# A one-core encoder layer: weights prepared twice are left out, two pairs share one raw tile, two sums move to VectorE

## The chip, the cores and the metric

The kernel runs on one core of one Trainium2 chip. The metric is the time of one execution on the device, in microseconds (us). Three executions of the kernel before took 1694.86, 1699.55 and 1696.46 us, so its median is 1696.46 us.

Five engines of the core have a part in it: TensorE (PE, matmuls, with its weight loads as PEld), VectorE (DVE), ScalarE (ACT), GpSimd (POOL) and SyncE (SP), which issues the DMAs. Each runs its own instructions strictly in their order and waits for others by semaphores.

## The reference

One layer of an encoder is computed for 1024 prompt rows and 128 sample rows (8 requests of 16): a mixer of a linear recurrence and a sliding-window attention, a cross attention into 256 memory tokens, and a feed-forward, each with a residual and a layer norm. The change touches only the last line of this:

```python
D_MODEL = 1024
D_FF = -(-8 * D_MODEL // (3 * 256)) * 256          # 2816

def swiglu(x, w_in, w_out):
    g, u = jnp.split(x @ w_in, 2, axis=-1)
    return (jax.nn.silu(g) * u) @ w_out

def post_blocks(x, mix, mk, mv, w_mem_q, w_mem_o, w_ffn_in, w_ffn_out, ln_g, ln_b):
    x = layer_norm(ALPHA * x + mix, ln_g[0], ln_b[0])
    x = layer_norm(ALPHA * x + mem_attention(x, mk, mv, w_mem_q, w_mem_o), ln_g[1], ln_b[1])
    x = layer_norm(ALPHA * x + swiglu(x, w_ffn_in, w_ffn_out), ln_g[2], ln_b[2])
    return x
```

Everything is float32.

## The kernel before

**Precision.** A float32 operand is split into a high part (a cast to the fp32r format, on ACT) and a low part (the operand less the high part, a subtraction). A product is three matmuls: high by high, high by low, low by high (`mm3`). So each operand of TensorE costs a cast on ACT and a subtraction on DVE or POOL, of 128x512 elements in the part that matters here.

**The feed-forward in 2x2 blocks.** Both its projections use the scheme of Strassen and Winograd: a product of 2x2 blocks takes seven block products in place of eight, and additions ahead and behind. The second projection multiplies the hidden values (2816 wide) by `w_f2`. The 2816 rows are 11 *pairs* of 256. Pair i of `w_f2` is one raw tile, 128x2x1024, loaded in two DMAs of 512 KB (L1124); its blocks A11, A12, A21, A22 are 128x512 each. Four sums S1 to S4 of these blocks are made on POOL (L1135, in `add`). Eight blocks (A11, A12, A21, A22, S1 to S4) are then split: the cast on ACT (L1147, in `upper`), the low part on DVE, or on POOL for A21 and A22 (L1153, in `lower`). The low and high parts of a pair fill four tiles `w2`. All this is "the preparation of pair i"; the results stay in the dictionary `prepared` until they are used.

**The hidden values** come out of the first projection as seven operands, B11, T1, T2, B22, T3, B21 and T4, are stored to a scratch in DRAM (L1049), and are loaded back as tiles `hq` (L1198), whose split is `hh` (ACT, L1207) and `hl` (L1208; DVE, or POOL for T1, T3, T4). Their last differences are L1082 (POOL) and L1090 (DVE, for the last pair). The sample rows' hidden values have their own way: tanh on ACT (L961), two operations on DVE (L962, L963).

**Parts and turns.** `PARTS = ((0, 2), (2, 4), (4, 6), (6, 8), (8, 11))` groups the pairs: part 0 holds pairs 0 and 1, and so on, the last part pairs 8, 9 and 10. The prompt rows are eight tiles of 128; tile b (0 to 3) and tile b+4 make the two rows of the 2x2 scheme, so there are four *blocks* of tiles. A part but the last runs a first *turn* over blocks 0 and 1, then the sample rows, then a second turn over blocks 2 and 3. The last part takes the blocks one at a time: 0, 1, the sample rows, 2, 3, and normalizes each block's rows as it ends (`final_norm`, L1095 to L1111). A turn runs seven steps, and each adds a product to a bank of PSUM:

```python
        steps = (("x", "A11", "B11", True, (0, 0, None)),
                 ("z", "S1", "T1", True, (1, 1, None)),
                 ("x", "S2", "T2", False, (1, 0, None)),
                 ("z", "S4", "B22", False, (1, 0, 1)),
                 ("x", "S3", "T3", False, (1, 1, 1)),
                 ("w", "A12", "B21", True, (0, 0, 0)),
                 ("x", "A22", "T4", False, (0, 1, 0)))
```

Behind each step an add on DVE (L1230) reads the bank into the result `y` and so frees the bank; the w products go through `tap` instead (ACT L1227, POOL L1228), except in the last part. There are two banks each of x, z, w and s (sample rows). TensorE cannot start a product into a bank that is not free.

**What is prepared when.** While part n runs, `plans` prepares the pairs of part n+1 in between. It returns two lists, `first` and `second`, one for each turn: what stands in slot z of a list is written behind step z of that turn. `put` fills them: `load` is the raw load, `a0` the sums S1 and S2, `a1` the sums S4 and S3, `u0` to `u3` the casts, `l0` to `l3` the low parts. In the last part the first of its two turns with a plan is block 1's. The framework then gives each engine its order, from the order in the code and its own view of when operands are ready; the rows below show what came out.

**Memory.** Pool `c` has 14 units of 128x2048 float32, shared by raw tiles, sums, `w2` tiles and a few others, and exists from the first projection on. Pool `f2` is opened with the second projection, over the memory of the first projection's tiles. It holds the results `y`, the `hq`, `hh` and `hl` tiles, and one raw tile, used by the second pair of each part (`k == 1` in `plans`). The raw tile of the first pair of each part is a unit of `c`, and may therefore be loaded before `f2` is there. A tile is loaded anew only when its last reader is through.

**One more thing in the last part.** Its branch loads the gains and offsets of the layer norm in a loop over `n`, the name that also numbers the parts:

```python
                for n in range(2):
                    nc.sync.dma_start(out=gb[n], in_=I["ln"][4 + n:5 + n, :].broadcast_to([P, D]))
            load_sample, part_sample, hx = sample_operands(part)
            first, second = plans(n, load_sample, part_sample)
```

Behind the loop n is 1, so `plans` works for part 2: pair 4 is loaded, summed and split once more, and pair 5's raw tile loaded once more. The last part doesn't use them, and `second` isn't run there.

The loads of `y` at the start are L1311, the store of the sample's hidden values L1314.

Of the kernel before, what the change touches and what calls it, by code (L numbers as in the profile page):

```python
# [18 lines left out]
P = 128  # L19
D = 1024  # L20
# [12 lines left out]
PAIRS = FT // 2  # L33
FILL = 5
PARTS = ((0, 2), (2, 4), (4, 6), (6, 8), (8, 11))
# [67 lines left out]
def trunk(ctx, tc, I, O):  # L103
    nc = tc.nc
    V, S, G = nc.vector, nc.scalar, nc.gpsimd
# [28 lines left out]
    def split(src, hi, lo, scale=None):  # L134
        if scale is None:
            S.copy(hi, src)  # L136
            V.tensor_tensor(lo, src, hi.bitcast(F32), op=ALU.subtract)  # L137
        else:
            S.activation(hi, src, AF.Copy, scale=scale)
            V.scalar_tensor_tensor(lo, src, scale, hi.bitcast(F32), op0=ALU.mult, op1=ALU.subtract)  # L140
# [88 lines left out]
    both = const.tile([P, 1280], F32, name="both")  # L229
# [689 lines left out]
    def unit(c, name, dt=F32):  # L919
        return c.tile([P, 2048], dt, name=name, tag="u", bufs=14)  # L920
# [192 lines left out]
    def second_weights(c):  # L1113

        prepared = {}

        def prepare(i, at):

            raw, sums, units, out = [], [], [], prepared.setdefault(i, {})

            def load():
                t = at().tile([P, 2, 1024], F32, name="raw2") if at else unit(c, "raw2").rearrange("p (n x) -> p n x", n=2)
                for n in range(2):
                    nc.sync.dma_start(out=t[:, n], in_=I["w_f2"][n, i])  # L1124
                raw.extend(t[:, n, x * 512:x * 512 + 512] for n in range(2) for x in range(2))

            def add(k):
                a11, a12, a21, a22 = raw
                if k == 0:
                    t = unit(c, "s2").rearrange("p (n x) -> p n x", x=512)  # L1130
                    sums.extend(t[:, n] for n in range(4))
                s1, s2, s3, s4 = sums
                for o, x, y, op in (((s1, a21, a22, ALU.add), (s2, s1, a11, ALU.subtract)),
                                    ((s4, a12, s2, ALU.subtract), (s3, a11, a21, ALU.subtract)))[k]:
                    G.tensor_tensor(o, x, y, op=op)  # L1135

            def names(k):
                a11, a12, a21, a22 = raw
                s1, s2, s3, s4 = sums
                return ((("A11", a11), ("S1", s1)), (("S2", s2), ("S4", s4)), (("S3", s3), ("A12", a12)),  # L1140
                        (("A22", a22), ("A21", a21)))[k]

            def upper(k):
                t = unit(c, "w2", F32R).rearrange("p (n x) -> p n x", x=512)
                units.append(t)
                for n, (_, src) in enumerate(names(k)):
                    S.copy(t[:, 2 * n], src)  # L1147

            def lower(k):
                t = units[k]  # L1150
                for n, (name, src) in enumerate(names(k)):
                    hi, lo = t[:, 2 * n], t[:, 2 * n + 1]
                    (G if name in ("A21", "A22") else V).tensor_tensor(lo, src, hi.bitcast(F32), op=ALU.subtract)  # L1153
                    out[name] = hi, lo

            return {"load": load, **{f"a{k}": (lambda k=k: add(k)) for k in range(2)},
                    **{f"u{k}": (lambda k=k: upper(k)) for k in range(4)},
                    **{f"l{k}": (lambda k=k: lower(k)) for k in range(4)}}

        def first_operands():  # L1160

            (i0, i1), out = PARTS[0], {}
            k = i1 - i0
            q = unit(c, "q2")[:, :k * 512].rearrange("p (o i b x) -> p o i b x", o=2, i=k, b=2)
            t = unit(c, "h2", F32R)[:, :k * 1024].rearrange("p (o y i b x) -> p o y i b x", o=2, y=2, i=k, b=2)
            for n, o in enumerate(OPS[:2]):
                nc.sync.dma_start(out=q[:, n], in_=h_dram[0, n, :, i0:i1])
                split(q[:, n], t[:, n, 0], t[:, n, 1])
                out[0, o] = [[(t[:, n, 0, i, b], t[:, n, 1, i, b]) for i in range(k)] for b in range(2)]
            return out  # L1170

        return prepared, prepare, first_operands

    def second_projection(f2, c, ahead, prepared, prepare):

        y = {}
        sums = [bank("s") for _ in range(2)]
        gb = []
# [14 lines left out]
        def load(n):  # L1193
            if n < len(wanted) and n not in loaded:
                i0, i1, bs, o = wanted[n]
                k, m, c = i1 - i0, len(bs), bs[0] % 2
                q = f2.tile([P, 512], F32, name="hq", bufs=5)[:, :k * m * P].rearrange("p (i b x) -> p i b x", b=m, x=P)
                nc.sync.dma_start(out=q, in_=h_dram[bs[0] // 2, OPS.index(o), :, i0:i1, c:c + m])  # L1198
                loaded[n] = q
# [81 lines left out]
        def plans(n, load_sample, part_sample):  # L1281


            first, second = [[] for _ in steps], [[] for _ in steps]
            first[2].append(load_sample)
            first[5].append(part_sample)
            if n + 1 < len(PARTS):
                nexts = [prepare(i, (lambda: f2) if k == 1 else None) for k, i in enumerate(range(*PARTS[n + 1]))]

                def put(plan, k, **at):  # L1290
                    for x, z in at.items():
                        plan[z].append(nexts[k][x])

                put(first, 0, load=0, a0=1, a1=2, u0=2, l0=3, u1=3, l1=4, u2=4, l2=5, u3=5, l3=6)
                put(first, 1, load=1)
                put(second, 1, a0=0, a1=0, u0=0, l0=1, u1=1, l1=2, u2=2, l2=3, u3=3, l3=4)
                if len(nexts) > 2:
                    put(second, 2, load=3, a0=5, a1=5, u0=5, l0=6, u1=6, l1=6, u2=6, l2=6, u3=6, l3=6)
            return first, second
# [4 lines left out]
        for n, part in enumerate(PARTS):  # L1304
            last = n == len(PARTS) - 1
            if n == 0:

                for k, (e, half) in enumerate(((0, 0), (1, 1), (1, 0), (0, 1))):
                    c2 = slice(half * 512, half * 512 + 512)
                    for b in range(2):  # L1310
                        nc.sync.dma_start(out=y[b, e][:, c2], in_=x2_dram[TILES[b + 4 * e]][:, c2])  # L1311
                    if k == 1:
                        load(0)
                nc.sync.dma_start(out=hs_dram[:, PAIRS - 1], in_=hs.rearrange("p (e t) -> p e t", e=2))  # L1314
            if last:
                both = unit(c, "ln_gb").rearrange("p (n x) -> p n x", n=2)
                gb = [both[:, n] for n in range(2)]
                for n in range(2):
                    nc.sync.dma_start(out=gb[n], in_=I["ln"][4 + n:5 + n, :].broadcast_to([P, D]))
            load_sample, part_sample, hx = sample_operands(part)  # L1320
            first, second = plans(n, load_sample, part_sample)
            for bs in ((0,), (1,)) if last else ((0, 1),):
                yield from blocks(part, bs, gb, first if bs[-1] == 1 else ())
            if n == 0:
                for e in range(2):
                    for b in range(2, 4):
                        nc.sync.dma_start(out=y[b, e], in_=x2_dram[TILES[b + 4 * e]])
            yield from sample(part, hx, n == 0, last)
            if last:
                ys = unit(c, "ys")[:, :1024]  # L1330
                nc.sync.dma_start(out=ys, in_=x2_dram[SAMPLE])
                bn = sm.tile([P, 2, 6], F32, name="bn", bufs=6)
                for half in range(2):
                    c2 = slice(half * 512, half * 512 + 512)
                    V.scalar_tensor_tensor(ys[:, c2], ys[:, c2], ALPHA, sums[half], op0=ALU.mult, op1=ALU.add)
                    V.bn_stats(bn[:, half], ys[:, c2])
                final_norm(ys, gb, bn, None, None)
                for b in (2, 3):
                    yield from blocks(part, (b,), gb)
                return  # L1340
            yield from blocks(part, (2, 3), gb, second)
# [211 lines left out]
```

## Time and profile before

| | us |
|---|---|
| median of three executions | 1696.46 |
| the profiled execution | 1701.0 |
| its span in the trace | 1699.2 |
| PE busy in the span | 1625.7 |
| first product of the second projection (PE, x, 12 matmuls) starts | 1381.49 |

The mean granted clock of TensorE over the span is 0.98 of full. The second projection takes the stretch from there to the end. A row of the timeline gives the start in us from the span's start, the duration, the engine, the line, the operation with output and inputs, the count, and in brackets how long the engine stood before it and what ended that. A row of windows gives the stretch and its length, then busy time and count of PE, PEld, DVE, ACT and POOL, that of SP's DMA issues, the granted clock of TensorE (1.00 is full), the busy share of the DMA engines and the GB/s. A row of groups gives the count, the busy time, the mean in ns, and the idle time before; a row that lists durations gives the shortest, median and longest of one instruction in ns, and the stretch over which they lie.

### The profile page before, as it was taken

How to read it: one execution, taken by the hardware profiler on the slowest of the kernel's cores; microseconds unless marked ns; L12 is line 12 of the kernel's file. 1: busy time of each engine (PE TensorE's matmuls, PEld its weight loads, DVE VectorE, ACT ScalarE, POOL GpSimd, SP SyncE). 2: the span in 40 equal slices, each digit the busy share in tenths (PEclk: the TensorE clock that was granted, in tenths of full speed). 3: DMA queues.
4: the chain of work that ended last, by engine and by line, in shares of the span. 5: the costliest groups of instructions: out<-in, count | busy, mean ns of one | idle time of the engine just before them, and what ended most of it. 6: DMA issues, size and time to landing. Idle time of an engine off the chain costs nothing.

```text
span 1699.2 us, 24497 instructions
## 1 busy us (share of the span) xinstructions
PE 1625.7 (96%) x9065; PEld 1397.4 (82%) x9065; DVE 1145.7 (67%) x2032; ACT 681.7 (40%) x1380; POOL 511.3 (30%) x389
## 2 busy tenths in 40 slices
PE   8999999999999999999999999999999979999894
PEld 7998999999888987889887888888888867777672
DVE  6886688788478666787687545544444576677766
ACT  4543455546433545134353333322322434334322
POOL 1111121111000000000057444323333455678556
PEclk9999999999999999999999999999999989999997
DMA  7453243333875588637364222322222256344431
GB/s 239 133 170 122 91 149 106 97 117 122 291 281 165 179 269 303 225 113 258 124 211 140 100 93 100 106 83 90 91 96 96 91 186 208 88 129 131 155 110 74
DMA packets 120679, 252.11 MB, mean 148 GB/s; under 512 B 12144, under 2 KB 63728, under 8 KB 120560
## 3 DMA queue, kind: packets, MB, share of 16 engines
q1 hardware_dynamic: 120560, 250.55, 44.3%
q8 instruction: 71, 1.16, 0.3%
q14 instruction: 48, 0.39, 0.1%
HBM read 207.84 MB, written 42.60 MB: 147 GB/s over the span
## 4 chain that ended last, share of the span: by engine, by line
PE 80%; DVE 7%; POOL 5%; DMA 4%; ACT 2%; issue 2%; SPq 1%; POOLq 0%; ACTq 0%; DVEq 0%
PE a L96 47%; PE b L96 20%; PE x L96 5%; PE z L96 3%; POOL s L1135 2%; PE b L100 2%; PE s L96 2%; DMA raw<-in_w_f_dram 2%; DVE w L1153 1%; PE w L96 1%; DVE T_l L940 1%; DMA w_raw<-in_w_mv_dram 1%; DVE sc L550 1%; DVE B_l L940 1%; DVE w_lo L137 0%
## 5 line engine op out<-in xcount | busy, mean ns | idle before, releaser
L137 DVE TENSOR_TENSOR w_lo<-w_raw,w_hi 128x1024 fp32r<-128x1024 f32 (+1 forms) x169 | 204.9, 1216 | 115.6 <-ACT w_hi L136 115.1
L136 ACT CAST w_hi<-w_raw 128x1024 fp32r<-128x1024 f32 (+1 forms) x169 | 174.5, 1035 | 207.4 <-PE a L96 76.8
L96 PE MATMUL a<-w_hi,q_hi 128*128 128x256 f32 (+1 forms) x576 | 197.6, 344 | 0.7 <-ACT kv_sb L270 0.7
L96 PE MATMUL a<-w_lo,q_hi 128*128 128x256 f32 (+1 forms) x576 | 196.9, 342 | 0.0
L96 PE MATMUL a<-w_hi,q_lo 128*128 128x256 f32 (+1 forms) x576 | 194.6, 338 | 0.0
L96 PE MATMUL a<-q_hi,w_hi 128*128 128x384 f32 x528 | 187.5, 355 | 6.1 <-ACT q_hi L136 4.1
L96 PE MATMUL a<-q_hi,w_lo 128*128 128x384 f32 x528 | 180.4, 342 | 0.0
L96 PE MATMUL a<-q_lo,w_hi 128*128 128x384 f32 x528 | 180.2, 342 | 0.0
L96 PE MATMUL x<-w,hh 128*128 128x512 f32 x344 | 115.0, 417 | 22.4 <-DVE y L1230 14.5
L137 DVE TENSOR_TENSOR w_lo<-a,w_hi 128x1024 fp32r<-128x1024 f32 x43 | 75.0, 1746 | 76.6 <-ACT w_hi L136 76.6
L96 PEld LDWEIGHTS a<-w_hi,q_hi 128*128 128x128 f32 x576 | 108.3, 188 | 15.0 <-ACT kv_sb L270 1.1
L96 PEld LDWEIGHTS a<-w_lo,q_hi 128*128 128x128 f32 x576 | 108.6, 189 | 13.4 <-issue 1.2
L96 PEld LDWEIGHTS a<-w_hi,q_lo 128*128 128x128 f32 x576 | 108.5, 188 | 13.3 <-issue 0.5
L96 PEld LDWEIGHTS a<-q_hi,w_hi 128*128 128x128 f32 x528 | 101.0, 191 | 11.9 <-ACT q_hi L136 5.3
L699 POOL TENSOR_TENSOR rs<-rs,mhalf 128x1 f32<-128x1 f32 x18 | 17.2, 958 | 302.9 <-DVE rs L698 302.9
L96 PE MATMUL a<-T_h,w_hi 128*128 128x512 f32 x264 | 104.7, 397 | 0.0
L96 PE MATMUL a<-T_h,w_lo 128*128 128x512 f32 x264 | 104.7, 396 | 0.0
L96 PE MATMUL a<-T_l,w_hi 128*128 128x512 f32 x264 | 104.6, 396 | 0.0
L96 PEld LDWEIGHTS a<-q_lo,w_hi 128*128 128x128 f32 x528 | 101.0, 191 | 2.0 <-DVE q_lo L137 0.9
L96 PEld LDWEIGHTS x<-w,hh 128*128 128x128 f32 x344 | 67.5, 199 | 42.7 <-issue 13.1
L96 PEld LDWEIGHTS a<-q_hi,w_lo 128*128 128x128 f32 x528 | 100.8, 191 | 1.0 <-DVE w_lo L137 0.4
L1207 ACT CAST hh<-hq 128x512 fp32r<-128x512 f32 (+1 forms) x82 | 47.3, 582 | 92.6 <-PE x L96 53.9
(308 smaller groups left out, 3975.6 us busy)
## 6 DMA issues: line engine op xcount, KB each, us to landing
a<-in_w_f_dram SPq DMA_DIRECT2D x44, 512.0 KB, 5.3
w_raw<-in_w_fm_dram SPq DMA_DIRECT2D x41, 512.0 KB, 4.0
h_scratch<-w_raw SPq DMA_DIRECT2D x55, 256.0 KB, 2.2
hq<-h_scratch SPq DMA_DIRECT2D x54, 256.0 KB, 3.3
raw<-in_w_f_dram SPq DMA_DIRECT2D x26, 512.0 KB, 4.5
w_raw<-in_w_tm_dram SPq DMA_DIRECT2D x24, 512.0 KB, 3.4
w_raw<-in_w_out_dram SPq DMA_DIRECT2D x24, 512.0 KB, 5.3
w_raw<-in_w_mq_dram SPq DMA_DIRECT2D x24, 512.0 KB, 4.3
```

The lines of the kernel that those rows point to most:

```text
L96: return self.eng.matmul(out, lhsT, rhs, **kw)
L100: return self.eng.transpose(out, in_, identity)
L136: S.copy(hi, src)
L137: V.tensor_tensor(lo, src, hi.bitcast(F32), op=ALU.subtract)
L550: V.tensor_tensor_reduce(sb[kv][:, j, :nk], pss[kv][:, j, :nk], swa_bias[:, head + j, 256 - nk:], scale=1.0, scalar=sinks[:, head + j:head ...
L699: G.tensor_tensor(rs, rs, mhalf[:, 0:1], op=ALU.pow)
L940: (G if o == "T4" else V).tensor_tensor(lo, b[o], hi.bitcast(F32), op=ALU.subtract)
L1135: G.tensor_tensor(o, x, y, op=op)
L1153: (G if name in ("A21", "A22") else V).tensor_tensor(lo, src, hi.bitcast(F32), op=ALU.subtract)
L1207: S.copy(hi, q)
```

## The change

There are three edits.

1. In the last part the loop over the gains and offsets is over `k`, so n stays 4, `n + 1 < len(PARTS)` is false there, and nothing is prepared.
2. While part 0 runs (n == 0), both pairs of part 1, pairs 2 and 3, take the one raw tile of `f2`. Pair 2 is loaded behind step 2 of the first turn and summed and split behind steps 4 to 6; pair 3 is loaded behind step 0 of the second turn and summed and split behind steps 1 to 6. Before, pair 2 took a unit of `c`, loaded behind step 0, and pair 3 was loaded behind step 1 of the first turn.
3. The sums S1 and S2 of the last pair, pair 10, are made on DVE instead of POOL.

```diff
@@ -1132,7 +1132,7 @@
                 s1, s2, s3, s4 = sums
                 for o, x, y, op in (((s1, a21, a22, ALU.add), (s2, s1, a11, ALU.subtract)),
                                     ((s4, a12, s2, ALU.subtract), (s3, a11, a21, ALU.subtract)))[k]:
-                    G.tensor_tensor(o, x, y, op=op)
+                    (V if i == PAIRS - 1 and k == 0 else G).tensor_tensor(o, x, y, op=op)
@@ -1285,15 +1285,19 @@
             if n + 1 < len(PARTS):
-                nexts = [prepare(i, (lambda: f2) if k == 1 else None) for k, i in enumerate(range(*PARTS[n + 1]))]
+                nexts = [prepare(i, (lambda: f2) if k == 1 or n == 0 else None) for k, i in enumerate(range(*PARTS[n + 1]))]
...
-                put(first, 0, load=0, a0=1, a1=2, u0=2, l0=3, u1=3, l1=4, u2=4, l2=5, u3=5, l3=6)
-                put(first, 1, load=1)
-                put(second, 1, a0=0, a1=0, u0=0, l0=1, u1=1, l1=2, u2=2, l2=3, u3=3, l3=4)
+                if n == 0:
+                    put(first, 0, load=2, a0=4, a1=4, u0=5, l0=5, u1=5, l1=6, u2=6, l2=6, u3=6, l3=6)
+                    put(second, 1, load=0, a0=1, a1=2, u0=2, l0=3, u1=3, l1=4, u2=4, l2=5, u3=5, l3=6)
+                else:
+                    put(first, 0, load=0, a0=1, a1=2, u0=2, l0=3, u1=3, l1=4, u2=4, l2=5, u3=5, l3=6)
+                    put(first, 1, load=1)
+                    put(second, 1, a0=0, a1=0, u0=0, l0=1, u1=1, l1=2, u2=2, l2=3, u3=3, l3=4)
@@ -1314,9 +1318,9 @@
             if last:
                 both = unit(c, "ln_gb").rearrange("p (n x) -> p n x", n=2)
-                gb = [both[:, n] for n in range(2)]
-                for n in range(2):
-                    nc.sync.dma_start(out=gb[n], in_=I["ln"][4 + n:5 + n, :].broadcast_to([P, D]))
+                gb = [both[:, k] for k in range(2)]
+                for k in range(2):
+                    nc.sync.dma_start(out=gb[k], in_=I["ln"][4 + k:5 + k, :].broadcast_to([P, D]))
```

The rows that follow are the instructions of one engine in the order in which it runs them: line, operation, output and inputs, size, and a count where the same row follows itself. Numbers behind `w_`, `s_` and `raw_` tell tiles of one name apart. In the changed kernel the lines behind `plans` stand four lower (L1311 is L1315, and so on).

ACT at the start of the second projection, before; `both` is the sample rows' tanh, the `w_` rows are pair 2's casts:

```order
L1043 ACTIVATE w_raw<-a 128x512
L1147 CAST w_13138<-raw_13079 128x512
L1147 CAST w_13138<-s_13098 128x512
L1147 CAST w_13163<-s_13098 128x512
L1147 CAST w_13188<-s_13098 128x512
L1147 CAST w_13163<-s_13098 128x512
L1147 CAST w_13188<-raw_13079 128x512
L1147 CAST w_13227<-raw_13079 128x512 x2
L961 ACTIVATE both<-b 128x256
```

The same place now:

```order
L1043 ACTIVATE w_raw<-a 128x512
L961 ACTIVATE both<-b 128x256
L1207 CAST hh<-hq 128x512 x4
L136 CAST hsh<-hs 128x256 x2
L1147 CAST w_13209<-raw_13127 128x512
L1147 CAST w_13209<-s_13170 128x512
```

Pair 2's eight casts stand behind the tanh and behind the first four `hq` casts, where they stood ahead of both.

DVE at the border of parts 3 and 4, before; tiles 14563, 14614, 14619, 14644 and 14649 are pair 10's raw tile, sums and split blocks:

```order
L1208 TENSOR_TENSOR hl<-hq,hh 128x384
L1153 TENSOR_TENSOR w_14619<-raw_14563,w_14619 128x512
L1153 TENSOR_TENSOR w_14619<-s_14614,w_14619 128x512
L1230 SCALAR_TENSOR_TENSOR y<-y,x 128x512
L1153 TENSOR_TENSOR w_14644<-s_14614,w_14644 128x512 x2
L1230 SCALAR_TENSOR_TENSOR y<-y,x 128x512
L1153 TENSOR_TENSOR w_14649<-s_14614,w_14649 128x512
```

The same place now:

```order
L1208 TENSOR_TENSOR hl<-hq,hh 128x384
L1135 TENSOR_TENSOR s_14614<-raw_14563 128x512
L1135 TENSOR_TENSOR s_14614<-s_14614,raw_14563 128x512
L1153 TENSOR_TENSOR w_14619<-raw_14563,w_14619 128x512
L1153 TENSOR_TENSOR w_14619<-s_14614,w_14619 128x512
L1230 SCALAR_TENSOR_TENSOR y<-y,x 128x512
L1153 TENSOR_TENSOR w_14644<-s_14614,w_14644 128x512 x2
```

The two sums stand on DVE ahead of the low parts and the adds that they stood behind on POOL's side.

POOL in the last part, before; tiles 14850, 14830 and 14973 belong to the second preparation of pair 4, `rs`, `y` and `ys` rows to the normalization of prompt and sample rows:

```order
L1106 TENSOR_TENSOR y<-y,ln_gb 128x512
L1208 TENSOR_TENSOR hl<-hq,hh 128x384 x3
L1135 TENSOR_TENSOR s_14850<-raw_14830 128x512 x2
L1135 TENSOR_TENSOR s_14850<-s_14850,raw_14830 128x512
L1135 TENSOR_TENSOR s_14850<-raw_14830,s_14850 128x512
L1153 TENSOR_TENSOR w_14973<-raw_14830,w_14973 128x512 x2
L1208 TENSOR_TENSOR hl<-hq,hh 128x384
L1099 TENSOR_TENSOR rs<-rs,mhalf 128x1 x2
L1105 TENSOR_TENSOR ys<-ys,ln_gb 128x512
```

The same place now:

```order
L1106 TENSOR_TENSOR y<-y,ln_gb 128x512
L1099 TENSOR_TENSOR rs<-rs,mhalf 128x1
L1105 TENSOR_TENSOR ys<-ys,ln_gb 128x512
L1106 TENSOR_TENSOR ys<-ys,ln_gb 128x512
L1208 TENSOR_TENSOR hl<-hq,hh 128x384 x2
L1099 TENSOR_TENSOR rs<-rs,mhalf 128x1
```

The six instructions of pair 4 are gone, and the sample rows' normalization (`ys`) stands ahead of the next two low parts.

## The prediction

> **What bounds the kernel now.** I read the page's totals first, then TensorE's timeline for its waits, then the engine that each wait names.
>
> ```profile
> span 1699.2 us, 24497 instructions
> PE 1625.7 (96%) x9065; PEld 1397.4 (82%) x9065; DVE 1145.7 (67%) x2032; ACT 681.7 (40%) x1380; POOL 511.3 (30%) x389
> ...
> 1392.65 2.90 PE L96 MATMUL z<-w,h 128*128 128x512 f32 x6 [6.80 <-DVE both L963]
> 1403.96 0.73 PE L96 MATMUL z<-w,hh 128*128 128x512 f32 x2 [3.67 <-ACT hh L1207]
> 1406.25 0.79 PE L96 MATMUL z<-w,hl 128*128 128x512 f32 x1 [1.55 <-DVE hl L1208]
> 1450.39 1.22 PE L96 MATMUL x<-w,hh 128*128 128x512 f32 x2 [2.75 <-DVE y L1230]
> 1499.92 0.73 PE L96 MATMUL x<-w,hh 128*128 128x512 f32 x2 [1.41 <-DVE y L1230]
> 1602.05 1.22 PE L96 MATMUL x<-w,hh 128*128 128x512 f32 x2 [5.40 <-DVE y L1230]
> 1622.66 0.70 PE L96 MATMUL z<-w,hh 128*128 128x512 f32 x2 [1.27 <-DVE y L1230]
> 1666.97 1.22 PE L96 MATMUL z<-w,hh 128*128 128x512 f32 x2 [4.02 <-DVE y L1230]
> 1681.18 1.19 PE L96 MATMUL x<-w,hh 128*128 128x512 f32 x2 [7.53 <-DVE rs L1098]
> ...
> 1425.70 2.81 PE x L96 x12
> 1602.00:1607.00 5.00, 4.95 (x12) 3.88 (x13) 3.25 (x5) 0.51 (x1) 1.54 (x2) 0.50 0.80 270
> ```
>
> PE works 96% of the span, so only time in which PE stands, or runs slowly, can be won. All large waits lie in the second projection, and the bracket at the end of each row gives the wait and its releaser: 6.80, 3.67 and 1.55 us at its start, 2.75 at the border of parts 0 and 1, 5.40 at the border of parts 3 and 4, 1.27, 4.02 and 7.53 in the last part. At full clock a matmul takes 2.81/12 = 0.234 us. After a long wait it is twice that: in the window behind the 5.40 us wait the clock column (0.50) says so. The row at 1450.39 spends 1.22 us on two matmuls after a 2.75 us wait, the one at 1499.92 only 0.73 after 1.41: the clock falls somewhere between those waits. A fall costs about 2 us, four or five microseconds at half speed.
>
> **Term 1: the start.** Who holds PE there?
>
> ```profile
> 1374.42 7.31 PE L96 MATMUL b<-both,a 128*128 128x128 f32 x64
> 1384.33 1.52 PE L96 MATMUL z<-w,h 128*128 128x512 f32 x6
> 1383.54 0.62 ACT L1147 CAST w<-s 128x512 fp32r<-128x512 f32 x1 [4.82 <-POOL s L1135]
> 1391.22 0.38 ACT L961 ACTIVATE both<-b 128x256 f32<-128x256 f32 x1
> 1385.24 1.76 DVE L1090 TENSOR_TENSOR w_raw<-w_raw,m 128x512 f32<-128x512 f32 x1
> 1380.98 1.27 POOL L1082 TENSOR_TENSOR w_raw<-w_raw 128x512 f32<-128x512 f32 x1
> 1382.28 5.11 SPq L1049 DMA_DIRECT2D h_scratch<-w_raw  x3
> 1387.48 1.86 SPq L1311 DMA_DIRECT2D y<-x_scratch  x4
> 1395.29 0.62 ACT L1207 CAST hh<-hq 128x512 fp32r<-128x512 f32 x1 [3.69 <-DMA hq<-h_scratch]
> 1395.29 1.97 SPq L1198 DMA_DIRECT2D hq<-h_scratch  x3
> 1410.88 3.56 PE x L96 x12
> h_scratch<-w_raw SPq DMA_DIRECT2D x55, 256.0 KB, 2.2
> raw<-in_w_f_dram SPq DMA_DIRECT2D x26, 512.0 KB, 4.5
> ```
>
> The sample's products end at 1374.42 + 7.31 = 1381.7, but their tanh (L961) runs on ACT only at 1391.22, because eight casts of pair 2 stand ahead of it and the second of them waits 4.82 us for POOL's sums. DVE's L1090, whose result SP stores before it may load y, is held in the same way until 1385.24, and the store holds SP's queue for 5.11 us. The change moves pair 2 behind all this. L961 then runs at about 1381.8 and DVE's L962 and L963 end near 1383.3, before PE needs the bank at 1384.33 + 1.52 = 1385.85: **the 6.80 us wait goes**, and the z products end at 1387.2.
>
> What is late next is the first hq (T2). L1090 needs POOL's difference that ends at 1381.0, so it ends by 1382.9 even if it takes its 1.76 us. The stores follow at 1382.3 to 1383.1 and y after the landing of the store ahead of the last (2.2 us in the page's list of DMA issues): 1384.9 instead of 1387.48, 2.6 us earlier. The y loads and that hq keep their distances, so the cast at 1395.29 comes at 1392.7 and PE goes on at 1393.4. It stands 6.2 us and pays one fall of the clock: the 12 products of S2 end near 1398.0. B22's hq was issued at 1395.29 (SP's row) behind the 1 MB of pair 3's raw; now no raw lies ahead of it, it goes out near 1391.4 and lands before 1398. So the waits of 3.67 and 1.55 us and the second slow stretch go: S4 ends near 1400.8 instead of 1410.88, **10.1 us earlier**.
>
> Part of it is given back, because pair 3 now waits for the one raw tile.
>
> ```profile
> L1135 POOL TENSOR_TENSOR s<-raw 128x512 f32<-128x512 f32 x8 | 11.7, 1476 | 8.7 <-DMA raw<-in_w_f_dram 8.7
> L1228 POOL TENSOR_TENSOR y<-y,tap 128x512 f32<-128x512 f32 x4 | 6.0, 1503 | 4.2 <-ACT tap L1227 4.1
> L1153 POOL TENSOR_TENSOR w<-raw,w 128x512 fp32r<-128x512 f32 x6 | 9.3, 1565 | 4.1 <-ACT w L1147 4.1
> ```
>
> Pair 2's load goes out near 1395 and lands near 1400 (4.5 us is the page's median). POOL's four sums take 4 x 1.5 us, then T4's low part 1.4 (a difference of 512 columns like L1082 at 1.27 and the sums at 1.48), two tap adds 3.0, the two low parts 3.1: the raw tile is free near 1413.5 and pair 3 lands near 1418. The second turn, 14.8 us after S4's end now (1425.70 against 1410.88), starts near 1415.6. Pair 3's A11 and S1 then stand on DVE ahead of the adds of z, and S2 is summed only near 1423. DVE makes eight low parts between adds that PE waits for; I charge 2.4 us, between nothing (they were ready long before) and 6 (the sums last again), and 0.7 us for T4's low part. **Term 1: 10.1 - 3.1 = 7 us**, ends 2 and 11. The border to part 1 keeps its 2.75 us wait: pair 4's load still waits for the same products.
>
> **Term 2: the border of parts 3 and 4.** Now POOL makes the sums of pair 10, and DVE stands behind them.
>
> ```profile
> 1587.92 3.00 POOL L1135 TENSOR_TENSOR s<-raw 128x512 f32<-128x512 f32 x2 [1.51 <-DMA raw<-in_w_f_dram]
> 1594.53 2.93 DVE L1153 TENSOR_TENSOR w<-s,w 128x512 fp32r<-128x512 f32 x2 [2.47 <-ACT w L1147]
> 1601.32 0.67 DVE L1230 SCALAR_TENSOR_TENSOR y<-y,x 128x512 f32<-128x512 f32 x1
> L1153 DVE TENSOR_TENSOR w<-s,w x48: 684/1172/1780, 1347.9 to 1665.0; 128x512 fp32r<-128x512 f32 x48
> ```
>
> POOL starts at the landing, 1587.92, and puts a tap add ahead of S2's sum; DVE idles 2.47 us for it, then makes four low parts with an add between, and only then the add at 1601.32 that frees PE. With S1 and S2 on DVE from the landing at 1587.9 that idle time goes, but two more instructions of this kind come in. No row shows an L1135 on DVE; the nearest are L1153's: 0.68 at the shortest, 1.17 in the median, 1.78 at the longest. POOL works nearly all of this stretch, so I take 1.4. Eight in a row and two adds of 0.6 make 1587.9 + 8 x 1.4 + 1.2 + waits of 0.3 = 1600.6 against 1601.32: 0.7 us won. The ends are 8 x 0.8 (4.2 us more won) and 8 x 1.75 (2.1 us lost). The first add (A22, block 2) now has four of the eight ahead of it instead of two and comes some 2.5 us later, so PE stands once for 2 to 2.6 us and once for some 3 instead of 5.40: the fall of the clock may lie in the second wait, or be paid. **Term 2: 1.5 us**, ends -3 and +6.
>
> The Trainium skill speaks against this edit: its page "SBUF — State Buffer", section "Who interferes with whom", says that a DVE instruction with two SBUF inputs and a GpSimd instruction that reads SBUF lock each other out for a whole instruction. By that rule the sums would only change places on one port and the term would be nothing or a loss; the trace's 0.68 to 1.78 us agree with the lock, and the rival below is worked out from rows.
>
> **Term 3: the last part.** The preparation left out is pair 4's (plans is called with n = 1 there), whose products are long done.
>
> ```profile
> 1663.08 2.64 DVE L1153 TENSOR_TENSOR w<-s,w 128x512 fp32r<-128x512 f32 x3 [1.84 <-ACT w L1147]
> ...
> 1684.73 0.63 PE L96 MATMUL x<-w,hl 128*128 128x512 f32 x1
> 1694.72 1.26 POOL L1106 TENSOR_TENSOR y<-y,ln_gb 128x512 f32<-128x512 f32 x1
> ...
> 1630.94 0.39 PE L96 MATMUL x<-w,hl 128*128 128x512 f32 x1
> 1634.64 1.46 POOL L1208 TENSOR_TENSOR hl<-hq,hh 128x384 fp32r<-128x384 f32 x1
> 1639.09 1.28 POOL L1106 TENSOR_TENSOR y<-y,ln_gb 128x512 f32<-128x512 f32 x1
> ...
> 1607.00:1623.00 16.00, 14.73 (x64) 11.58 (x63) 12.99 (x24) 4.83 (x9) 8.15 (x8) 1.00 0.54 183
> ```
>
> It goes: four sums and two low parts on POOL, eight casts on ACT, six low parts on DVE, and four loads of 512 KB. The 4.02 us wait (DVE's adds stand behind these low parts) and the 7.53 us wait (behind the sample rows' normalization, which came late into the same queue) go with their two falls of the clock. Added up from the border: PE goes on at 1601.3, at half clock for half of the usual stretch (+1), with 0.7 us for B22's low part; then 36 matmuls of block 0, 63 of each other block and 36 of the sample, 261 x 0.234 = 61.2 us after the first nine (2.1). For waits I add 1.3 in block 1 and 1.3 in block 3 (the row at 1622.66, next to the same normalization) and 0.8 in block 2 for the sample rows. Sum: 1601.3 + 1 + 2.1 + 0.7 + 61.2 + 3.4 = 1669.7, against 1684.73 + 0.63 = 1685.36: 15.7 us, in which term 2 is counted (its 0.7 directly, its clock by the +1).
>
> The end behind PE shortens too. Block 1's products ended at 1631.3 and its last L1106 at 1640.4, 9.1 us later, of which 1.46 are a low part of the next block on POOL that block 3 doesn't have: 7.6. Block 3's took 1685.36 to 1695.98, 10.6. The 3.2 us from there to the span's end stay. I take 7.9, so 2.7 us less. **Terms 2 and 3 together: 15.7 + 2.7 = 18.4 us**, ends 10 and 24.
>
> **The sum.** 7 + 18.4 = 25.4 us. The profiled execution took 1701.0 us, 1.8 more than its span; it would take 1675.6. The median of the runs shown lies 4.5 below it, so the forecast is 1696.46 - 25.4 = **1671**.
>
> **Rivals.** *One raw tile is too few* (A): pair 3 lands after 1421, every DVE add of the second turn waits for a low part, and the start's 10.1 us are eaten. Against it: 2 to 3 us of room in the chain above; for it: seven steps in which POOL is late by what DVE's neighbours cost. Terms 2 and 3 stay: 1696.5 - 18.4 = 1678 to 1681. *The lock at the border* (B): the eight instructions take 1.75 us each, PE goes on at 1604 and slowly: 2.1 + 1.2 lost instead of 1.5 won, 1676. *DVE becomes the bound of the last part* (D): between 1607 and 1623 it was busy 12.99 of 16 us without any low part of weights, and its normalization, which waits for POOL, already cost 1.27. Were it 3 us in each of the three later blocks instead of 3.4 in all, 5.6 more: 1677. *Slower* (C): the same raw tile as in A, but pair 3's second load stuck so long that part 1 starts without its weights. From a landing near 1447, 29 us later than above, the loss passes the 25.4 won; at 1455 it gives 1704. Nothing in SP's new order puts a late wait ahead of that load. That the change does nothing is excluded by the order of instructions: the sums, casts and loads are gone from it.
>
> **How the numbers follow.** Forecast 0.64, A 0.12, D 0.12, B 0.07, C 0.03, more won than forecast 0.02. With both low ends (2 and 10) 1684, with both high (11 and 24) 1661; the range is 1661 to 1683. All cases but C are faster by over 0.3% (5 us, about what this measurement can tell from no change): faster 0.95, same 0.02, slower 0.03.
>
> **What would show it.** Right: L961 near 1382, z's second group without a wait, no second wait before S4, L1135 twice on DVE, no L1147 after 1640, PE without waits over 2 us in the last part and ending near 1663 on the trace's clock. Wrong: waits on DVE's adds between 1415 and 1435 (A), a wait over 5 us at the border (B), or three waits of 3 us in the last part (D).

## The result and the profile after

| | before | changed |
|---|---|---|
| median, 4 executions each | 1698.01 us | 1678.55 us (1673.07 to 1686.94) |
| ratio, with its 95% interval | | 0.9891 (0.9844 to 0.9938) |
| profiled execution | 1701.0 us | 1680.5 us |
| its span | 1699.2 us | 1678.6 us |
| granted clock over the span | 0.980 | 0.986 |

The change wins 19.5 us where 25.4 were forecast; the time lies in the range, 7.5 us above the forecast. The profiled executions differ by 20.5 us, of which 1.26 are a head start: the second projection's first product starts at 1380.23 instead of 1381.49. The change has no part in that: e1 below, which leaves everything ahead of it alone, starts at 1377.38.

First the page's head and TensorE's timeline of the changed kernel, the rows with the larger waits at the start, at the borders and in the last part (columns as before; waits of 1.23 and 1.41 us at the border of parts 1 and 2 are left out).

```profile
span 1678.6 us, 24469 instructions
PE 1619.6 (96%) x9065; PEld 1392.9 (83%) x9065; DVE 1144.6 (68%) x2028; ACT 675.8 (40%) x1372; POOL 502.1 (30%) x381
...
1392.24 1.22 PE L96 MATMUL x<-w,hh 128*128 128x512 f32 x2 [6.28 <-ACT hh L1207]
1442.10 0.77 PE L96 MATMUL x<-w,hh 128*128 128x512 f32 x2 [4.57 <-DVE y L1230]
1447.94 1.22 PE L96 MATMUL x<-w,hh 128*128 128x512 f32 x2 [2.94 <-DVE y L1230]
1546.87 0.73 PE L96 MATMUL x<-w,hh 128*128 128x512 f32 x2 [2.75 <-DVE y L1230]
1594.50 0.70 PE L96 MATMUL x<-w,hh 128*128 128x512 f32 x2 [2.50 <-DVE y L1230]
1600.12 0.73 PE L96 MATMUL x<-w,hh 128*128 128x512 f32 x2 [1.17 <-DVE y L1230]
1619.03 0.70 PE L96 MATMUL z<-w,hh 128*128 128x512 f32 x2 [1.27 <-DVE y L1230]
1659.11 0.70 PE L96 MATMUL z<-w,hh 128*128 128x512 f32 x2 [1.26 <-DVE y L1230]
```

At the start one long wait, 6.28 us, is left of three. The last part has none over 1.27 behind its border. But at the border of parts 0 and 1, where PE waited 0.40 and 2.75 us before, it now waits 4.57 and 2.94 us. The table follows PE through the second projection: starts read off the timelines, less the start of its first product, so that the head start is out of it. The columns of the experiments are used below.

| us from the first product | before | changed | e1 | e2 | e3 | e5 | e10 |
|---|---|---|---|---|---|---|---|
| (the first product starts at) | 1381.49 | 1380.23 | 1377.38 | 1377.61 | 1378.51 | 1375.71 | 1378.72 |
| part 0, second turn starts | 44.04 | 36.26 | 43.51 | 35.00 | 42.59 | 34.60 | 34.50 |
| part 1, w products of the first turn start | 82.76 | 82.43 | 83.56 | 82.48 | 79.39 | 76.59 | 72.49 |
| part 3, w products of the second turn start | 204.32 | 205.99 | 205.91 | 206.04 | 203.47 | 200.51 | 192.25 |
| last part, block 2 starts | 258.12 | 255.74 | 260.00 | 258.87 | 252.87 | 249.57 | 241.50 |
| last product ends | 303.87 | 287.54 | 291.80 | 304.38 | 298.42 | 281.38 | 273.31 |

Between before and changed: 7.8 us are won by the second turn of part 0 (44.04 - 36.26); all but 0.3 of them are lost again by the first turn of part 1; another 2.0 go by part 3, where the clock fell behind the wait of 2.75 us; the border of parts 3 and 4 brings 4.1 (from 1.67 behind to 2.38 ahead), the last part 13.9, and the end behind PE 3.0 (1699.2 - 1685.36 = 13.8 against 1678.6 - 1667.77 = 10.8). With the head start that is the 20.6 us between the spans.

### The profile page after: what moved, and what is told of

Its sections match the earlier page's. It is cut to its first block, busy times and chain, and to the rows that moved or that the text cites. A ratio compares the mean times of both kernels' runs of the same rounds, so it can differ in the third digit from the quotient of the medians.

```text
span 1678.6 us, 24469 instructions
## 1 busy us (share of the span) xinstructions
PE 1619.6 (96%) x9065; PEld 1392.9 (83%) x9065; DVE 1144.6 (68%) x2028; ACT 675.8 (40%) x1372; POOL 502.1 (30%) x381
## 4 chain that ended last, share of the span: by engine, by line
PE 80%; DVE 7%; DMA 5%; POOL 4%; issue 2%; ACT 2%; SPq 0%; POOLq 0%; DVEq 0%; ACTq 0%
PE a L96 48%; PE b L96 21%; PE x L96 4%; PE z L96 3%; PE b L100 2%; DMA raw<-in_w_f_dram 2%; POOL s L1135 2%; PE s L96 2%; DVE w L1153 1%; DVE y L1230 1%; DMA w_raw<-in_w_f_dram 1%; PE w L96 1%; DMA w_raw<-in_w_mv_dram 1%; ACT w_hi L136 1%; DMA hq<-h_scratch 1%
```

## The experiments

All medians stand beside runs of the kernel before on the same chip; kernels of one group share them.

| kernel | median | before beside it | ratio (95% interval) |
|---|---|---|---|
| e1, third edit alone | 1678.84 | 1696.87 | 0.9900 (0.9884 to 0.9916) |
| e2, second edit alone | 1697.27 | 1696.87 | 1.0009 (0.9995 to 1.0023) |
| e3, first edit alone | 1693.37 | 1696.87 | 0.9977 (0.9964 to 0.9990) |
| e4, changed, adds ahead of pair 4 | 1676.28 | 1696.87 | 0.9898 (0.9876 to 0.9921) |
| e5, changed, pair 3 in a unit of its own | 1670.92 | 1694.97 | 0.9857 (0.9834 to 0.9880) |
| e6, e4 and adds ahead of two more low parts | 1673.05 | 1694.97 | 0.9863 (0.9841 to 0.9884) |
| e7, e6 at three borders | 1669.22 | 1694.97 | 0.9838 (0.9816 to 0.9860) |
| e8, the changed kernel again | 1677.35 | 1694.97 | 0.9892 (0.9871 to 0.9914) |
| e9, e5 and e7's order at the later borders | 1668.41 | 1698.31 | 0.9829 (0.9812 to 0.9846) |
| e10, e5 and e7 | 1665.39 | 1698.31 | 0.9816 (0.9800 to 0.9832) |

### One edit at a time: e1, e2, e3

Each is the kernel before with one hunk of the change's diff and nothing else: e1 the loop over `k`, e2 the hunk of `plans`, e3 the line with `V if i == PAIRS - 1 and k == 0`.

> The kernel before with the third edit alone: the last part prepares nothing. Theory: the last part's gain stands on its own, since the changed kernel was 3.6 us ahead of before when block 2 began and 20.6 us at the end: 17 us less than before (15 to 19), PE waits of 4.02 and 7.53 us gone from the last part, the border of parts 3 and 4 as before (a wait of about 5.4 us with a fall of the clock). Rival: a part of those 17 us came from the border's sums on DVE or from the earlier start; then 10 to 13 us.

> The kernel before with the second edit alone: pairs 2 and 3 from the one raw tile, pair 2 later. Theory: the second turn of part 0 starts 7 to 9 us earlier than before, but at the border of parts 0 and 1 the adds that free PE's banks stand on DVE behind the low part of pair 4's A11, whose load lands only some 4 us earlier; PE waits 4 to 5 us there and again about 3 us, and at the end 0 to 3 us are left. Rival (the sum of the prediction): the long wait at that border was this one execution's, and 6 to 8 us are left at the end.

> The kernel before with the first edit alone: S1 and S2 of pair 10 on DVE. Theory: the one wait of 5.4 us at the border of parts 3 and 4 becomes two of 2.5 and 1.2 us, too short for the clock to fall, and 4 us are won (3 to 5). Rival (the prediction): a fall of the clock is still paid in half of the cases, 1.5 us. Rival (port lock): eight instructions of 1.75 us on DVE, PE goes on 2 us later than before, 2 to 3 us lost.

Rows of PE's timeline: of e1 at the border of parts 3 and 4,

```profile
1599.30 1.22 PE L96 MATMUL x<-w,hh 128*128 128x512 f32 x2 [5.41 <-DVE y L1230]
```

of e2 at the border of parts 0 and 1,

```profile
1440.25 1.19 PE L96 MATMUL x<-w,hh 128*128 128x512 f32 x2 [4.53 <-DVE y L1230]
1446.09 1.22 PE L96 MATMUL x<-w,hh 128*128 128x512 f32 x2 [2.52 <-DVE y L1230]
```

and of e3 at the border of parts 3 and 4.

```profile
1590.31 0.71 PE L96 MATMUL x<-w,hh 128*128 128x512 f32 x2 [2.55 <-DVE y L1230]
```

e1 wins 18.0 us by the medians (14.3 to 19.7 by the interval): the last part's gain stands on its own, with the border ahead of it still at 5.41 us and no wait over 1.28 us behind it. e3 wins 3.5 (1.7 to 6.1), the theory's amount rather than the prediction's 1.5. But the theory's reason failed: only one wait stands at the border, 2.55 us, and behind it the clock did fall (0.76 of full over the next 7 us). e2 wins nothing that can be measured (0.8 won to 3.9 lost), though its second turn of part 0 starts 9.0 us earlier (44.04 - 35.00): the same long waits stand at the border, so they were not one execution's, and there the 9 us shrink to 0.3 (82.76 - 82.48). The three shares add up to the whole: 1.00 - 0.09 + 0.23 = 1.14% against 1.09% of the changed kernel, inside the intervals. So the question is what takes the start's gain at that border.

### What stands there

SP's queue, POOL, ACT and DVE of the changed kernel at the border of parts 0 and 1, by time within each engine (s of L1153 is a sum of pair 4 that POOL made):

```profile
1415.81 0.81 SPq L1124 DMA_DIRECT2D raw<-in_w_f_dram  x2
1430.48 0.34 SPq L1198 DMA_DIRECT2D hq<-h_scratch  x1
1430.92 7.83 SPq L1124 DMA_DIRECT2D raw<-in_w_f_dram  x4
...
1429.16 1.29 POOL L1208 TENSOR_TENSOR hl<-hq,hh 128x512 fp32r<-128x512 f32 x1 [0.59 <-ACT hh L1207]
...
1437.66 0.62 ACT L1147 CAST w<-raw 128x512 fp32r<-128x512 f32 x1 [1.13 <-DMA raw<-in_w_f_dram]
...
1438.31 1.38 DVE L1153 TENSOR_TENSOR w<-raw,w 128x512 fp32r<-128x512 f32 x1 [1.53 <-ACT w L1147]
1439.61 1.75 DVE L1208 TENSOR_TENSOR hl<-hq,hh 128x512 fp32r<-128x512 f32 x1
1441.28 0.67 DVE L1230 SCALAR_TENSOR_TENSOR y<-y,x 128x512 f32<-128x512 f32 x1
...
1446.08 1.20 DVE L1153 TENSOR_TENSOR w<-s,w 128x512 fp32r<-128x512 f32 x1 [3.05 <-ACT w L1147]
1447.21 0.68 DVE L1230 SCALAR_TENSOR_TENSOR y<-y,x 128x512 f32<-128x512 f32 x1
```

and of before, SP, DVE and the first of PE's two waits:

```profile
1436.27 3.91 SPq L1124 DMA_DIRECT2D raw<-in_w_f_dram  x4
...
1442.55 0.78 DVE L1153 TENSOR_TENSOR w<-raw,w 128x512 fp32r<-128x512 f32 x1 [1.41 <-ACT w L1147]
1443.25 1.78 DVE L1208 TENSOR_TENSOR hl<-hq,hh 128x512 fp32r<-128x512 f32 x1
1444.95 0.68 DVE L1230 SCALAR_TENSOR_TENSOR y<-y,x 128x512 f32<-128x512 f32 x1
...
1449.66 0.68 DVE L1230 SCALAR_TENSOR_TENSOR y<-y,x 128x512 f32<-128x512 f32 x1
...
1445.77 0.70 PE L96 MATMUL x<-w,hh 128*128 128x512 f32 x2 [0.40 <-DVE y L1230]
```

The two L1230 free the banks that part 1's first products need. In both kernels the low part of pair 4's A11 (the first L1153) stands ahead of the first of them on DVE, and low parts of pair 4's sums ahead of the second. So PE goes on when pair 4 has landed and is summed, not when PE is ready. By the times of the two traces, head start and all, PE came to this border 7.9 us earlier than before (1437.53 against 1445.38), pair 4's load went out 5.4 earlier (1430.92 against 1436.27), the first add ran 3.7 earlier (1441.28 against 1444.95) and the second 2.5 (1447.21 against 1449.66). What PE gained it stood, most of it in the first wait.

The load went out later than it had to. Before, it left as a z product of the second turn ended (1436.24). In the changed kernel the same product ended at 1427.34, but the load stood on SP's queue right behind the hq load of 1430.48, which waited for a low part on POOL (1429.16 + 1.29); an hq load ahead of that had waited 7.0 us for another low part, which POOL made behind pair 3's sums.

### The order of DVE, or pair 3's lateness: e4 to e8

e4 keeps the program and moves pair 4's low parts behind the last add of part 0 on DVE, and its casts behind B22's cast on ACT. `tail[0]` holds the last L1230 written so far, `cast` the last cast of each operand; `issue_after` fixes the order on one engine and adds no wait.

```diff
+                def late(step, behind):
+                    with tc.issue_after(behind().ins):
+                        step()
+
+                if n == 1:
+                    add = tail[0]
+                    for x in range(4):
+                        nexts[0][f"l{x}"] = lambda step=nexts[0][f"l{x}"]: late(step, lambda: add)
+                        nexts[0][f"u{x}"] = lambda step=nexts[0][f"u{x}"]: late(step, lambda: cast["B22"])
```

> The changed kernel, with one place reordered: at the border of parts 0 and 1 DVE's low parts of pair 4 are queued behind the two last adds of part 0, and ACT's casts of pair 4 behind the cast of B22. Theory: those adds were late only because they stood behind pair 4's landing, so the waits of 4.57 and 2.94 us there go (none over 1.5 us left), the clock doesn't fall there, and it takes 7 to 9 us less than the changed kernel. Rival: the adds are late because DVE and POOL are slow at that place, each instruction 1.2 to 1.8 us in place of 0.7; then a wait of 3 us or more stays, and 0 to 3 us are won.

DVE and PE of e4 at the border:

```profile
1436.54 3.31 DVE L1208 TENSOR_TENSOR hl<-hq,hh 128x512 fp32r<-128x512 f32 x2 [0.97 <-ACT hh L1207]
1439.77 1.27 DVE L1230 SCALAR_TENSOR_TENSOR y<-y,x 128x512 f32<-128x512 f32 x2
...
1440.60 0.70 PE L96 MATMUL x<-w,hh 128*128 128x512 f32 x2 [3.10 <-DVE y L1230]
```

Both adds now run together, and the second wait is gone. But two low parts of hq (of T2 and B22), 3.31 us for the two, still stand ahead of them and keep 3.10 us of the first; two smaller waits, 1.68 and 1.33 us, come up behind. The ratio, 0.9898, is that of the changed kernel (0.9891, 0.9892). The theory's 7 to 9 us fell. The rival's condition held: a wait over 3 us stayed, and the two low parts took 1.65 us each, where one of them took 0.69 in the changed kernel.

Next, e5 leaves the order to the framework and takes pair 3's wait away: pair 2 keeps f2's raw tile, pair 3 gets a unit of c.

```diff
-                nexts = [prepare(i, (lambda: f2) if k == 1 or n == 0 else None) for k, i in enumerate(range(*PARTS[n + 1]))]
+                nexts = [prepare(i, (lambda: f2) if (k == 1) != (n == 0) else None) for k, i in enumerate(range(*PARTS[n + 1]))]
```

> The changed kernel, but pair 3's raw tile is a unit of pool c again (pair 2 keeps the raw tile of f2), so pair 3's load no longer waits for pair 2's last reads. Theory: the start's gain was lost at the border of parts 0 and 1 because pair 3 came late (its load waited 13.1 us): POOL's sums, the low part that SP's hq loads wait for, and so pair 4's load and landing were late behind it. Pair 3 then lands some 10 us earlier, no wait over 3 us is left at that border, and 4 to 6 us less than the changed kernel. Rival: only the order on DVE (the low part of pair 4's A11 and two low parts of hq ahead of the two last adds) sets that border, whenever pair 3 comes; the waits stay at 4.5 and 2.9 us and the time within 1.5 us of the changed kernel.

e6 takes e4 and puts the two low parts of hq behind the adds too (`tail[1]` is the last add of part 0); e7 does this at the borders 0/1, 1/2 and 2/3 (`n > 0`, and every part but the last).

```diff
-                (G if o in ("T1", "T3", "T4") else V).tensor_tensor(lo, q, hi.bitcast(F32), op=ALU.subtract)
+                low = lambda: (G if o in ("T1", "T3", "T4") else V).tensor_tensor(lo, q, hi.bitcast(F32), op=ALU.subtract)
+                if o in ("T2", "B22") and tail[1] is not None:
+                    with tc.issue_after(tail[1].ins):
+                        low()
+                else:
+                    low()
```

> The kernel e4_adds_first with one more place reordered: at the border of parts 0 and 1 DVE's low parts of T2 and B22 of part 1 also stand behind the two last adds of part 0. Theory: the 3.10 us that PE still waited there in e4 were these two low parts (3.31 us on DVE ahead of the adds), so no wait over 1 us is left at that border, and it takes 2 to 4 us less than e4. Rival: the waits only move: what DVE does later is late for the next products, and the time stays within 1.5 us of e4.

> The order of e6 at the borders of parts 0/1, 1/2 and 2/3. Theory: the waits of 1.2 to 2.75 us at the two later borders have the same cause (the next preparation's low part ahead of the last adds) and go too: 3 to 6 us less than e6, so 1667 to 1671. Rival: they move into the turn behind, and the time stays within 1.5 us of e6.

> The changed kernel once more, beside the three above. Every theory: 1676 to 1680; the waits at the border of parts 0 and 1 are again above 4 and near 3 us. A rival that they were one execution's: a first wait under 2 us there.

e8 shows the border as before it: waits of 4.53 and 2.68 us. Against e8, on the same chip, e5 takes 6.4 us less, e6 4.3 and e7 8.1. The rows of e5 at the border (SP's load of pair 3 ahead of it, DVE and PE):

```profile
1397.08 1.76 SPq L1124 DMA_DIRECT2D raw<-in_w_f_dram  x2
...
1430.72 0.62 ACT L1147 CAST w<-raw 128x512 fp32r<-128x512 f32 x1 [1.42 <-DMA raw<-in_w_f_dram]
...
1432.98 0.67 DVE L1230 SCALAR_TENSOR_TENSOR y<-y,x 128x512 f32<-128x512 f32 x1
1433.58 1.16 DVE L1153 TENSOR_TENSOR w<-raw,w 128x512 fp32r<-128x512 f32 x1
...
1436.36 0.67 DVE L1230 SCALAR_TENSOR_TENSOR y<-y,x 128x512 f32<-128x512 f32 x1
...
1437.09 0.73 PE L96 MATMUL x<-w,hh 128*128 128x512 f32 x2 [1.42 <-DVE y L1230]
```

Pair 3's load goes out at 1397.08, 21.4 us behind the first product, where the changed kernel has 35.6 (1415.81 - 1380.23). No wait over 1.66 us is left at the border. The time came out as the theory had it, its chain only in part. Counted from the first product, pair 4's load goes out no earlier (51.3 against 50.7), but its first cast, which waits for the landing, comes 3.7 us behind it instead of 6.7, and so 2.4 us earlier (55.0 against 57.4). The two adds come 3.8 and 6.3 us earlier (57.3 against 61.1, 60.7 against 67.0). The rest is order: with pair 3 out of the way the framework puts the first add ahead of A11's low part, and POOL's tap adds ahead of pair 4's sums. How much of the 6.4 us is the earlier landing and how much the order, e5 does not separate.

e6 has no wait over 0.3 us at the border any more, but a new one of 4.76 us in part 1. By the ratios it is still 5.9 us ahead of e4 (0.9863 against 0.9898, with intervals that overlap), where 2 to 4 were expected. e7 has the new wait too:

```profile
1441.01 0.62 ACT L1147 CAST w<-s 128x512 fp32r<-128x512 f32 x1 [4.48 <-POOL s L1135]
...
1446.14 0.82 DVE L1208 TENSOR_TENSOR hl<-hq,hh 128x512 fp32r<-128x512 f32 x1 [5.72 <-ACT hh L1207]
...
1447.62 1.22 PE L96 MATMUL z<-w,hh 128*128 128x512 f32 x2 [4.76 <-DVE y L1235]
```

A cast of hq stands on ACT behind pair 4's casts, which wait 4.48 us for POOL's sums; DVE's low part waits 5.72 for it, with an add behind it that PE waits for. So the rival of e6, that waits move on, held for one wait, but not in the time. At the two later borders of e7 only 0.67 and 0.83 us are left, and it is 3.8 us ahead of e6: those waits had the same cause, as expected.

### Both together: e9, e10

e9 is e5 with e7's order at the borders 1/2 and 2/3 alone (`n > 1`, `PARTS[2:-1]`), e10 is e5 with all of e7.

> e5 (pair 3's raw tile a unit of c) with the order of e7 at the borders of parts 1/2 and 2/3 alone; the border of parts 0/1 as in e5. Theory: both gains add up, e5's 6 us at the first border and some 3 us at each of the two later ones less what moves on: 3 to 6 us less than e5, near 1666, with no wait over 1 us at the borders 1/2 and 2/3. Rival: with pair 3 early the later borders run differently and their waits move behind the border; within 1.5 us of e5.

> e5 with the order of e7 at all three borders. Theory: as e9, and the first border's three waits of 1.4 us go too, but the wait of 4.76 us that e7 has in part 1 (a low part on DVE whose cast stands on ACT behind pair 4's casts, which wait for POOL's sums) comes with that order: within 2 us of e9 in either direction. Rival: pair 4 now lands earlier, so its casts don't hold ACT and that wait doesn't come; then 3 us less than e9.

PE's timeline of e10, its waits over 0.2 us between the start and the border of parts 3 and 4:

```profile
1433.65 0.74 PE L96 MATMUL x<-w,hh 128*128 128x512 f32 x2 [1.40 <-DVE y L1235]
...
1446.32 0.73 PE L96 MATMUL z<-w,hh 128*128 128x512 f32 x2 [0.75 <-DVE y L1235]
1455.01 0.70 PE L96 MATMUL x<-w,hh 128*128 128x512 f32 x2 [0.83 <-DVE y L1235]
1501.66 0.70 PE L96 MATMUL x<-w,hh 128*128 128x512 f32 x2 [0.83 <-DVE y L1235]
1548.18 0.70 PE L96 MATMUL x<-w,hh 128*128 128x512 f32 x2 [0.83 <-DVE y L1235]
```

Against the runs of before beside them e5 wins 24.1 us, e9 29.9 and e10 32.9. The gains add up, as the theory of e9 had it; for e10 its rival was right: with pair 4 early the wait of 4.76 us is down to 0.75, though one of the first border's three waits of 1.4 us stays. The intervals of e5, e9 and e10 overlap, so the steps between them rest on the waits in the traces more than on the medians. e10 is the version that beats both kernels: it takes 1.84% less than before and, ratio against ratio, some 13 us less than the changed kernel.

## Why the prediction was right, and where not

**The start** went as written, up to the border. On the changed kernel's clock (1.26 us earlier):

```profile
1380.51 0.39 ACT L961 ACTIVATE both<-b 128x256 f32<-128x256 f32 x1 [5.51 <-PE b L96]
1391.57 0.62 ACT L1207 CAST hh<-hq 128x512 fp32r<-128x512 f32 x1 [10.67 <-DMA hq<-h_scratch]
...
1419.68 0.62 ACT L1147 CAST w<-raw 128x512 fp32r<-128x512 f32 x1 [7.68 <-DMA raw<-in_w_f_dram]
```

L961 runs as soon as its products end, and 12 z products run through. The first cast of hq comes at 1391.57 (1392.7 forecast, less 1.26: 1391.4), PE goes on at 1392.24 (1392.1). S4 had no second long wait. The slow stretch cost 3 us instead of 2 (12 products of S2 took 5.3 us instead of 2.8, and z still ran slowly), so 8.3 instead of 10.1 us were won by the end of S4. Pair 3 landed near 1419.7, 3 us later than forecast on this clock and just at rival A's limit (1421 on the clock of before). Yet less was given back than the 3.1 us charged. With the head start taken off, 8.3 us ahead became 7.8 by the start of the second turn (PE waited 1.09 us for T4's low part, where 0.7 was charged, but the slow stretch of before had still 0.8 us to cost) and 6.7 at its T4 (1.1 lost, where 2.4 was charged). So the term's 7 us were there when PE reached the border, by two misses that nearly cancel.

**The step that failed** is one sentence: "The border to part 1 keeps its 2.75 us wait: pair 4's load still waits for the same products." It took PE's wait for a property of the border. A wait is the difference of two arrivals: PE's moved by 6.6 us (head start taken off), the first add's by 2.4. The sentence also left out that PE waits there twice. The 2.75 us stayed nearly as they were, 2.94, but the 0.40 us ahead of them became 4.57, with a longer slow stretch; 6.7 us ahead became 0.3. Nor did the load wait for the same: the product had ended 3.6 us before the load went out, behind SP's hq loads, which pair 3's late work held. With this term at zero (e2) instead of 7, the forecast would have been 1678, where the time is. That it lies so close is luck: the 2.6 us that term 2 won beyond its size and the 2.0 lost at the border of parts 2 and 3 nearly cancel. 1678 is also the price of rival A, which had a chance of 0.12 and named a cause that e5 bears out, the one raw tile, but another place: within the second turn of the changed kernel PE waited 0.22 us at most for an add. In e2, e4, e6 and e7, also with the one raw tile, it waited there once, 1.31 to 1.76 us.

**Term 2** was mis-sized: 4.1 us in the profile and 3.5 in e3, inside its ends of -3 and +6. DVE at the border of parts 3 and 4 in the changed kernel:

```profile
1587.99 0.69 DVE L1135 TENSOR_TENSOR s<-raw 128x512 f32<-128x512 f32 x1 [0.41 <-DMA raw<-in_w_f_dram]
1588.72 1.67 DVE L1135 TENSOR_TENSOR s<-s,raw 128x512 f32<-128x512 f32 x1
1590.31 1.78 DVE L1153 TENSOR_TENSOR w<-raw,w 128x512 fp32r<-128x512 f32 x1
1592.02 1.74 DVE L1153 TENSOR_TENSOR w<-s,w 128x512 fp32r<-128x512 f32 x1
...
1594.28 1.77 DVE L1153 TENSOR_TENSOR w<-s,w 128x512 fp32r<-128x512 f32 x2
...
1596.57 1.20 DVE L1153 TENSOR_TENSOR w<-s,w 128x512 fp32r<-128x512 f32 x1
1597.69 1.78 DVE L1153 TENSOR_TENSOR w<-raw,w 128x512 fp32r<-128x512 f32 x1
1599.39 0.68 DVE L1230 SCALAR_TENSOR_TENSOR y<-y,x 128x512 f32<-128x512 f32 x1
```

The eight took 10.6 us (the row with x2 counts both), 1.33 each where 1.4 was taken, and the add that frees PE starts 11.4 us behind the landing, 13.4 before (1601.32 - 1587.92): 2.0 won instead of 0.7. The other 2 us are the fall of the clock, charged by half, which this execution did not pay. That was luck, but little hung on it: e3 and e8 paid it (0.76 of full over the 7 us behind waits of 2.55 and 2.57 us) and won 4.4 us at this border all the same, because at the lower clock PE reached the next bank after its add had run, so that the second wait (1.17 us here, some 3 in the forecast) is gone. The rule of the Trainium skill's page "SBUF — State Buffer", section "Who interferes with whom", shows in these rows (0.69 where POOL began its sum a moment later, 1.67 to 1.78 beside POOL), but what it would make of the time does not: the idle 2.47 us of DVE were worth more than the slower instructions cost.

**Term 3** held: 13.9 and 3.0 us, 17.0 in all with rounding, against 16.9 (18.4 less term 2); e1 has 18.0. No wait over 1.27 us was left (rival D would have three of 3), and no cast of weights runs behind 1595.7. PE ended at 1667.8 instead of near 1663: the start brought 6.7 us less than its term and the border of parts 2 and 3 took 2.0, against 2.6 more from term 2 and 1.3 of head start.

Two small sums of the prediction are off and move nothing: 261 x 0.234 is 61.1, and eight instructions at 0.8 us would win 4.8 us more, not 4.2.

## What to carry to other kernels

An engine that arrives earlier at a place where others set the time only waits longer there: before a gain is carried across such a place, write down when its releaser will come, and on what that depends. On an in-order engine, what frees a bank (an add) should stand ahead of what prepares the next stage, above all ahead of an instruction that waits for a load. And a late load in one stage can cost most where the engines that it delays are next needed, not where it lands.

## What the runs showed of the hardware

Behind waits of 2 to 2.8 us the clock fell in some cases and not in others. The windows of 7 us behind two waits of 2.75 and 2.76 us, of the changed kernel and of e8 (columns as before; the clock is the number behind POOL's):

```profile
1546.87:1553.87 7.00, 7.00 (x23) 5.57 (x24) 6.72 (x8) 3.67 (x7) 6.92 (x5) 0.76 0.29 76
```

```profile
1495.42:1502.42 7.00, 7.00 (x30) 5.67 (x31) 6.87 (x9) 3.82 (x7) 6.92 (x5) 1.00 0.28 75
```

The same wait was followed by a fall in one (7 us at 0.76 are 3.4 us at half clock) and by none in the other. Taken over the second projections of the 12 profiles, of the waits that began at full clock, two of 52 between 1.2 and 1.8 us were followed by a fall, and these two came right behind a longer wait; of 23 between 1.98 and 2.76 us 15 were; and all 26 from 3.10 us up. The Trainium skill's page "TensorE: Matmul & The Clock Gate", Part 1, has the clock drop after at least one idle window of about 3.4 us and come back after a busy one of the same length; the 3.4 us of this fall agree with the second, the waits of 1.98 to 2.76 us ahead of falls don't agree with the first. It is one reason why a border differs from run to run: the border of parts 2 and 3 cost the changed kernel 2.0 us more in this execution than it cost before, of which some 0.6 are longer waits (0.40 and 2.75 us against 1.19 and 1.39) and the rest the clock.
